# Two of a two-layer encoder's modulation vectors, moved: one from the attention to the channel mixer's first product, one from there to its second product

## Chip, cores and metric

The kernel runs on one core of a Trainium2 chip. The metric is device time in microseconds (us); the median of the runs is given. Batch 1, 1024 tokens, model width 1024, everything in float32. Matrix products are made exact to about float32 by splitting each operand into a high and a low part in a rounded format (`float32r`) and adding three products (high x high, high x low, low x high).

## The reference, cut to what matters

Two layers; layer 0 mixes tokens by forgetting attention, layer 1 by gated linear attention (GLA). Each layer has six modulation vectors of 1024 numbers, made from the one conditioning vector `c`:

```python
c_act = jax.nn.silu(c)
for i in range(DEPTH):
    mod = c_act @ ada_w[i] + ada_b[i]          # 1 x 6144, a 1024 x 6144 matrix per layer
    sh1, sc1, g1, sh2, sc2, g2 = jnp.split(mod, N_MOD, axis=-1)
    h = modulate(rms_norm(x, norm1_g[i]), sh1, sc1)
    y = mixer(h)                               # layer 0: attention, layer 1: GLA
    x = x + g1[:, None, :] * y
    h = modulate(rms_norm(x, norm2_g[i]), sh2, sc2)
    x = x + g2[:, None, :] * swiglu(h, ffn_w_in[i], ffn_w_out[i])
return rms_norm(x, final_g)
```

The vectors are numbered j = 0 to 5 in this order (shift, scale and gate of the token mixer, then shift, scale and gate of the channel mixer). Each is a product of one row with a 1024 x 1024 matrix, 4 MB of weights for very little arithmetic.

## The kernel before, in words

**Stages.** The kernel is one straight program: transposes and the first norm; the attention, by pairs of heads (eight pairs, `attention`), with the projections of the next pair woven in; the attention's output projection; layer 0's channel mixer; GLA; its output projection; layer 1's channel mixer; the last norm. TensorE (PE) carries the products, ScalarE (ACT) makes high parts and exponentials, VectorE (DVE) makes low parts, sums and maxima, GpSimd (POOL) scales and adds, and every DMA is issued from SyncE's queue (SP). Each engine works through its queue in order. The order in each queue is made by a scheduler at build time, from the order in which the program emits the operations and a simulated timeline.

**The channel mixer** (`ffn`, called for each layer) is made with a seven-product (Strassen) scheme. Its first product goes through 22 groups of columns; `prod` makes one of a group's seven block products. Its second product goes through three parts (`OC = 3`) of the hidden width, each with four column groups of seven products; `part` loads the hidden tiles of the next part from DRAM in between, and `late_raw` gives the buffers for those of them that have to be split into high and low parts on the chip (T3, T4). In the second product seven PSUM banks take results, which ScalarE or VectorE sums up (L1696, L1698).

**A modulation vector** is made by `ada_steps`, beside other work. With `nt` rows per partition a step loads a piece of the matrix by four DMAs (L423) and adds `nt` rows, each scaled by one number of `silu(c)`, onto an accumulator by VectorE (L442 the first, L444 the others, 128 x 256 each); after the last step TensorE sums over partitions (L449) and VectorE adds the bias (L452). With `nt` = 4 (attention) a vector has 8 steps of four operations and 32 DMAs of 128 KB; with `nt` = 2 (elsewhere) 16 steps of two operations and 64 DMAs of 64 KB. Either way it is 32 operations. `ahead` is how many steps are loaded in advance, which is the number of buffers less one; in the attention it is 0, with a ring of three buffers (`wr`) shared with the weights.

**When a step is emitted** is decided by a `Pace`: the surrounding code calls it with an amount of work just emitted (for instance `ada1(0.64 * n)` after each block product), and it emits steps until their stated costs have used the amount up. The cost of a step is 1.0 in the attention; elsewhere it is `ADA_A` between the load and the operations and `ADA_B` behind them. In the attention `ada0(3.3)` stands at the end of `qk_proj` for the head pairs from 2 on (12 calls). Before the change the vectors are made at these places:

- layer 0, vectors 0 and 1: before the attention, by other code
- layer 0, vectors 2, 3, 4, 5: attention
- layer 1, vectors 0 and 1: layer 0's channel mixer, first product (`mid`, three buffers)
- layer 1, vectors 2, 3, 4: GLA
- layer 1, vector 5: layer 1's channel mixer, first product

Other lines that are spoken of: L1138 adds the decay to the scores and takes the running extreme, L1142 the exponential, L1143 the reciprocal of the sum, L1144 the scaling of the probabilities, L1164 their transposes; L765, L767, L779 and L780 move projected queries and keys out of PSUM; L175 makes the low part of a weight block (`o_s`) or of probabilities; L286 to L288 are the three products of a split pair; L825 loads weights of the channel mixer, L1607 and L1597 hidden tiles.

Of the kernel before, what the change touches and what calls it, by code (L numbers as in the profile page):

```python
# [20 lines left out]
HALF = 512  # L21
# [32 lines left out]
def trunk(ctx, tc, x, c, ada_w, ada_b, norm1_g, norm2_g, ffn_w_in, ffn_w_out,  # L54
# [124 lines left out]
    opr_ = {}  # L179
# [131 lines left out]
    xr = Ring(big, take(8))  # L311
# [62 lines left out]
    for t in range(6):  # L374
        nt, src = (4, rows2[0:8, :]) if t < 4 else (2, crow)
# [35 lines left out]
    def ada_steps(l, j, acc, raw_of, nt, ahead):  # L411


        steps, got = deque(range(32 // nt)), deque()

        def load():
            if not steps:
                return
            n = steps.popleft()
            raw = raw_of([P, nt * 256], F32, f"ada{l}{j}{n}").rearrange("p (t c) -> p t c", t=nt)  # L420
            src = ada_w[l, 32 * nt * n:32 * nt * (n + 1), j * D:(j + 1) * D]
            for q in range(4):
                nc.sync.dma_start(raw[32 * q:32 * q + 32],  # L423
                                  src[:, 256 * q:256 * q + 256].rearrange("(r t) c -> r t c", t=nt))
            got.append(raw)

        for _ in range(ahead):
            load()
        for n in range(32 // nt):
            load()  # L430
            if ahead:
                yield ADA_A
            raw = got.popleft()
            with ExitStack() as es:
                if ahead:
                    es.enter_context(tc.issue_after(last_of("D")))
                elif n == 0:
                    es.enter_context(tc.issue_after(split_after["D"]))
                for t in range(nt):
                    o = (0 if nt == 4 else 32) + t * (32 // nt) + n  # L440
                    if n == t == 0:
                        nc.vector.tensor_scalar(acc, raw[:, t], c42[:, o:o + 1], None, op0=ALU.mult)  # L442
                    else:
                        nc.vector.scalar_tensor_tensor(acc, raw[:, t], c42[:, o:o + 1], acc,  # L444
                                                       op0=ALU.mult, op1=ALU.add)
            yield ADA_B if ahead else 1.0
        mp = pj([P, 2, 4], F32, f"mp{l}{j}")
        for b in range(2):
            nc.tensor.matmul(mp[:, b], acc[:, psl(b)], four, start=True, stop=True)  # L449
        o = l * 48 + j * 8  # L450
        qb = lambda t: t.rearrange("p (q b) -> p b q", b=2)
        nc.vector.tensor_add(qb(modc[:, l, j]), mp, qb(vec[:, o:o + 8]))  # L452
        for i, jj in ((0, 1), (1, 4)):
            if j == jj:
                make_a(l, i)
        yield 1.0
# [22 lines left out]

    ada0, ada1 = Pace(), Pace()  # L480

    def ada1_queue(js, acc, raws_):
        r = Cycle(raws_)
        for j in js:
            ada1.q.append(ada_steps(1, j, acc, r, 2, len(raws_) - 1))

    mk = mrows[2]
    nc.vector.memset(mk, 0.0)
# [608 lines left out]
    def qk_proj(p, i):  # L1097

        if i == 0:
            qkt[p] = qk_tiles(p)  # L1100
        wt = feed.next()
        feed.depth = 3
        for hf in range(2):
            ps = pj([P, HALF], F32, f"qk{i}{p}{hf}")
            yield from proj(ps, wt, hT, hf)
            (k_evac if i else q_evac)(ps, qkt[p], hf)
        if p > 1:
            ada0(3.3)

    oTs = {}  # L1110

# [108 lines left out]
            yield from g  # L1220

    acc0 = acc_r([P, 2, HALF], F32, "acc0")[:, 0, 0:256]
    for j in (2, 3, 4, 5):
        ada0.q.append(ada_steps(0, j, acc0, wr, 4, 0))
    run(v_half(0, 0, gates_end))
    q_evac(accs[1][1][1], qkt[0], 1)
# [76 lines left out]
    oh = new_h("oh")  # L1303
# [35 lines left out]
        def __init__(self, kind, i):  # L1339
            self.kind, self.i = kind, i  # L1340

    def ffn(l, oh, xs, slots, nm, mid, norm_end, each=None):

# [13 lines left out]
        b = {}  # L1357
# [217 lines left out]
        NSP = len(tsl) - 7 * OD  # L1575
        assert NSP == 3 * OD
        early_raw = Cycle([xs[k][:, hsl(hf)] for k in (6, 7) for hf in range(2)])
        late_raw = Cycle(list(tmpv) + [opr_["u"][0]])
        o = [{} for _ in range(OC)]
        ONAMES = ("B11", "T1", "T2", "T3", "B21", "T4", "B22")  # L1580

# [45 lines left out]
        def load_xr(i):  # L1627
            for a in range(2):
                for hf in range(2):
                    xr[(a, hf)] = late_raw()  # L1630
                    nc.sync.dma_start(xr[(a, hf)], x_sp[2 * i + a][:, hsl(hf)])

        nxt, n_nxt = [None], [0]
# [6 lines left out]
        for X in gs[2:]:  # L1640
            up = lambda n: advance(n) if X is gs[-1] else None
            if X is gs[-2]:
                ada1.flush()
                nxt[0] = part(0)
                advance(4)
            nc.scalar.copy(dest(X, C11), prod(feed.next(), B11))
            p5 = prod(feed.next(), T1)
            up(8)
            add(X, C12, prod(feed.next(), T2), C11)
            up(11)  # L1650
            add(X, C11, prod(feed.next(), B21))
            fin(X, C11)
            add(X, C22, prod(feed.next(), T3), C12)
            add(X, C12, p5)
            up(15)
            add(X, C21, prod(feed.next(), T4), C22)
            fin(X, C21)
            add(X, C22, p5)
            fin(X, C22)
            up(20)  # L1660
            add(X, C12, prod(feed.next(), B22))
            fin(X, C12)
            up(21)
# [4 lines left out]
            zs[i] = big.tile([P, 2, HALF], F32, tag=slots["to"][i], name=f"z{l}{i}")  # L1668
        for c_ in range(OC):
            last = c_ == OC - 1  # L1670
            n_nxt[0] = 0
            nxt[0] = last_part() if last else part(c_ + 1)
            for i in range(4):
                Y1, Y3 = (xs[2 * i][:, hsl(hf)] for hf in range(2))
                Y2, Y4 = (xs[2 * i + 1][:, hsl(hf)] for hf in range(2))
                Z1, Z5 = zs[i][:, 0], zs[i][:, 1]
                if last and i == 3:
                    feed.depth = 3

# [79 lines left out]
            marks["G0"] = last_of("G")  # L1759
        return gates  # L1760

    def mid(*js):
        v = Views(slots["hid"], 2, [HALF], f"ad{js[0]}").v
        ada1_queue(js, v[0][:, 0:256], v[1:4])

    ADA_A, ADA_B = 6.0, 3.0
    ffn(0, oh, xs, slots, "fo", lambda: mid(0, 1), norm_mixer)
    h1 = hs1
    after_norm = marks.pop("G0")
    split_after.update(marks)  # L1770
# [17 lines left out]
    athl = Ring(big, take(1))  # L1788
    s_slot, on_slot = take(2)
    ada_v = Views(take(2), 2, [HALF], "ad").v  # L1790
    ada1_queue((2, 3, 4), ada_v[0][:, 0:256], ada_v[1:3])
    ADA_A, ADA_B = 2.6, 1.0
    rm = ada_v[3]
    nc.vector.memset(rm, 1.0)
# [305 lines left out]
        return fzs[0]()  # L2100

    ADA_A, ADA_B = 12.0, 6.0
    ffn(1, oh, xs, slots, "go", lambda: mid(5), final_norm, final_scale)
    dump("xb1", xs)

# [28 lines left out]
```

## Time and profile before

| | |
|---|---|
| median of 3 runs | 2395.52 us (2395.1 to 2399.87) |
| the profiled execution's own time | 2397.77 us |
| its span, first to last instruction | 2396.1 us |
| mean granted clock of TensorE | 0.997 |
| data moved by DMA | 363.42 MB, 152 GB/s over the span |

The profile is of one execution, so sums are made against its 2397.77 us and then set against the median. In its lines a group is named by the line of the kernel, the engine, the operation, and output<-inputs by tile names without buffer numbers; PEld is TensorE's weight load, which overlaps its products. In a list of waits the numbers are us in total, times, longest. A wait for several things is put down to the one that came last. Matmuls overlap in the pipeline, so that their durations add up to more than TensorE's busy time.

### The profile page before, as it was taken

The numbers are of one execution on the slowest core, as the hardware profiler recorded it, in microseconds if no ns is written. First come the engines' busy times: TensorE is split into PE (matmuls) and PEld (weight loads), VectorE is DVE, ScalarE is ACT, GpSimd is POOL, SyncE is SP. The second block draws the span as 40 slices with busy tenths as digits, with TensorE's granted clock in tenths as the row PEclk, the third lists the DMA queues.
The fourth block names the chain that finished last, engine by engine and source line by source line (L and its number), as shares of the span: only waits on it lengthen the run. The fifth ranks groups of instructions, "written<-read, shape, count | busy, mean of one in ns | idle before, by whom it ended". The sixth has DMA issues, their size and how long they took to land.

```text
span 2396.1 us, 35784 instructions
## 1 busy us (share of the span) xinstructions
PE 2368.3 (99%) x12344; PEld 2016.8 (84%) x12344; DVE 1776.6 (74%) x3016; ACT 1127.8 (47%) x2164; POOL 1008.5 (42%) x911
## 2 busy tenths in 40 slices
PE   8999999999999999999999999999999999999998
PEld 7888888888888888888888888898888888888888
DVE  6577878886698788876798666655687877775787
ACT  6666555674443333345325645353343333345326
POOL 1333333333445666643264321222345666643262
PEclk9999999999999999999999999999999999999999
DMA  7422424342435544557655242334424544457664
GB/s 254 145 89 90 131 84 128 106 138 83 150 109 173 179 166 165 171 196 261 229 187 162 67 119 80 107 112 135 136 96 161 183 145 159 154 182 256 228 202 146
DMA packets 335773, 363.42 MB, mean 152 GB/s; under 512 B 24348, under 2 KB 277432, under 8 KB 335592
## 3 DMA queue, kind: packets, MB, share of 16 engines
q1 hardware_dynamic: 335592, 361.15, 45.9%
q8 instruction: 97, 1.59, 0.3%
q14 instruction: 84, 0.69, 0.1%
HBM read 268.19 MB, written 92.86 MB: 151 GB/s over the span
## 4 chain that ended last, share of the span: by engine, by line
PE 90%; DVE 5%; DMA 2%; ACT 1%; issue 1%; POOL 0%; SPq 0%; DVEq 0%; POOLq 0%; ACTq 0%
PE p_b L288 16%; PE p_b L286 16%; PE p_b L287 16%; PE t_b L1164 2%; PE o_b L1178 2%; PE qk_b L286 2%; PE qk_b L287 2%; PE qk_b L288 2%; PE vps_b L286 1%; PE vps_b L288 1%; PE vps_b L287 1%; PE s_b L1132 1%; PE s_b L1133 1%; PE gr_b L286 1%; PE gr_b L287 1%
## 5 line engine op out<-in xcount | busy, mean ns | idle before, releaser
L175 DVE TENSOR_TENSOR o_s<-xv_s,o_s 128x512 fp32r<-128x512 f32 (+1 forms) x376 | 324.1, 867 | 66.1 <-ACT o_s L174 65.6
L174 ACT CAST o_s<-xv_s 128x512 fp32r<-128x512 f32 (+1 forms) x376 | 216.2, 587 | 303.6 <-PE p_b L288 248.0
L287 PE MATMUL p_b<-B,o_s 128*128 128x512 f32 x608 | 237.8, 391 | 0.0
L288 PE MATMUL p_b<-B,o_s 128*128 128x512 f32 x608 | 237.5, 391 | 0.0
L286 PE MATMUL p_b<-B,o_s 128*128 128x512 f32 x608 | 236.3, 392 | 0.0
L1144 POOL TENSOR_SCALAR lp_s<-lp_s,st 128x128 f32<-128x128 f32 (+7 forms) x128 | 99.0, 778 | 291.1 <-DVE st L1143 280.7
L843 POOL TENSOR_TENSOR ex_s<-xv_s,xv_s 128x512 f32<-128x512 f32 (+1 forms) x64 | 85.5, 1335 | 292.8 <-DMA xv_s<-in_ffn_w_in_dram 120.7
L286 PE MATMUL p_b<-T,o_s 128*128 128x512 f32 x480 | 186.7, 389 | 0.0
L287 PE MATMUL p_b<-T,o_s 128*128 128x512 f32 x480 | 186.7, 389 | 0.0
L288 PE MATMUL p_b<-T,o_s 128*128 128x512 f32 x480 | 181.2, 389 | 0.0
L287 PEld LDWEIGHTS p_b<-B,o_s 128*128 128x128 f32 x608 | 115.0, 189 | 23.9
L286 PEld LDWEIGHTS p_b<-B,o_s 128*128 128x128 f32 x608 | 115.0, 189 | 23.8
L288 PEld LDWEIGHTS p_b<-B,o_s 128*128 128x128 f32 x608 | 114.7, 189 | 24.0
L1142 ACT ACTIVATE lp_s<-lp_s,st 128x128 f32<-128x128 f32 (+7 forms) x128 | 99.3, 777 | 65.2 <-DVE st L1138 62.1
L174 ACT CAST pt_s<-t_b 128x512 fp32r<-128x512 f32 (+1 forms) x160 | 79.7, 547 | 75.4 <-PE t_b L1164 73.9
L845 POOL TENSOR_TENSOR xv_s<-ex_s,xv_s 128x512 f32<-128x512 f32 (+1 forms) x64 | 88.1, 1377 | 60.7 <-DVE o_s L175 58.2
L1521 DVE TENSOR_TENSOR ex_s<-ex_s,p_b 128x512 f32<-128x512 f32 x140 | 93.7, 681 | 23.4 <-PE p_b L288 23.2
L227 POOL TENSOR_TENSOR w_l_s<-w__s,w_h_s 128x256 fp32r<-128x256 f32 x90 | 69.7, 803 | 94.7 <-ACT w_h_s L223 56.7
L175 DVE TENSOR_TENSOR pt_s<-t_b,pt_s 128x512 fp32r<-128x512 f32 (+1 forms) x160 | 96.2, 631 | 15.9 <-ACT pt_s L174 15.3
L287 PEld LDWEIGHTS p_b<-T,o_s 128*128 128x128 f32 x480 | 90.1, 188 | 18.7
L286 PEld LDWEIGHTS p_b<-T,o_s 128*128 128x128 f32 x480 | 90.1, 188 | 18.7
L288 PEld LDWEIGHTS p_b<-T,o_s 128*128 128x128 f32 x480 | 90.1, 188 | 18.6
(1954 smaller groups left out, 7392.9 us busy)
## 6 DMA issues: line engine op xcount, KB each, us to landing
xv_s<-in_ffn_w_in_dram SPq DMA_DIRECT2D x176, 256.0 KB, 3.3
hid_B<-x SPq DMA_DIRECT2D x70, 512.0 KB, 2.6
ad_s<-in_ada_w_dram SPq DMA_DIRECT2D x384, 64.0 KB, 2.4
hid_T<-x SPq DMA_DIRECT2D x36, 512.0 KB, 2.8
xv_s<-in_ffn_w_out_dram SPq DMA_DIRECT2D x96, 192.0 KB, 5.3
ada_s<-in_ada_w_dram SPq DMA_DIRECT2D x128, 128.0 KB, 2.8
xv_s<-in_ffn_w_out_dram SPq DMA_DIRECT2D x40, 256.0 KB, 2.9
T2o<-hid_T SPq DMA_DIRECT2D x18, 512.0 KB, 8.4
```

Source lines behind the costliest of these rows:

```text
L174: nc.scalar.copy(hi, src)
L175: nc.vector.tensor_sub(lo, src, hi.bitcast(F32))
L227: (nc.gpsimd if i < 3 else nc.vector).tensor_sub(lo[:, cs], rw[:, cs], hi[:, cs].bitcast(F32))
L286: nc.tensor.matmul(ps, ah, bh, start=start, stop=False)
L287: nc.tensor.matmul(ps, ah, bl, start=False, stop=False)
L288: nc.tensor.matmul(ps, al, bh, start=False, stop=stop)
L843: nc.gpsimd.tensor_add(s1, a21, a22)
L845: nc.gpsimd.tensor_sub(a11, s1, a11)
L1142: nc.scalar.activation(lp, lp, AF.Exp, bias=mcur, scale=-1.0, accum_out=st[:, qi, 2:3])
L1144: nc.gpsimd.tensor_scalar(lp, lp, st[:, qi, 3:4], 1.0, op0=ALU.mult, op1=ALU.mult)
L1164: nc.tensor.transpose(tp[:, i, :], lps[qi][:, psl(2 * b + jj)], ident)
L1521: nc.vector.tensor_add(d, d if src is None else dest(G, src), ps)
```

## The change

Layer 0's vector 5 (the gate of the channel mixer) goes from the attention's queue to the queue of layer 0's first product, layer 1's vector 1 from that queue to a new one in the second product, and the attention's pace goes from 3.3 to 2.4 a call. The new queue has one buffer and so loads nothing ahead; its accumulator and its buffer are the two halves of `opr_["u"]`, of which `late_raw` used one half before and no longer does (`load_xr`, later, uses it as before). It starts with the last two groups of the first product, at a pace of 5.0 and 2.5, and what is left is emitted before the last part of the second product. The conditions on `ahead` become conditions on `nt`, which is the same for all other vectors. `ffn` gets the new argument only for layer 0; the smaller `late_raw` holds in both layers.

```diff
-            if ahead:
+            if nt == 2:
                 yield ADA_A
...
-                if ahead:
+                if nt == 2:
                     es.enter_context(tc.issue_after(last_of("D")))
...
-            yield ADA_B if ahead else 1.0
+            yield ADA_B if nt == 2 else 1.0
...
-    def ada1_queue(js, acc, raws_):
+    def ada1_queue(ljs, acc, raws_):
         r = Cycle(raws_)
-        for j in js:
-            ada1.q.append(ada_steps(1, j, acc, r, 2, len(raws_) - 1))
+        for l, j in ljs:
+            ada1.q.append(ada_steps(l, j, acc, r, 2, len(raws_) - 1))
...
         if p > 1:
-            ada0(3.3)
+            ada0(2.4)
...
-    for j in (2, 3, 4, 5):
+    for j in (2, 3, 4):
         ada0.q.append(ada_steps(0, j, acc0, wr, 4, 0))
...
-        late_raw = Cycle(list(tmpv) + [opr_["u"][0]])
+        late_raw = Cycle(list(tmpv))
+        xr_raw = Cycle(list(tmpv) + [opr_["u"][0]])
...
             if X is gs[-2]:
                 ada1.flush()
+                if later:
+                    ada1_queue(later, opr_["u"][1][:, 0:256], opr_["u"][0:1])
+                    ada_rate(5.0, 2.5)
...
             last = c_ == OC - 1
+            if last:
+                ada1.flush()
...
-    ffn(0, oh, xs, slots, "fo", lambda: mid(0, 1), norm_mixer)
+    ffn(0, oh, xs, slots, "fo", lambda: mid((0, 5), (1, 0)), norm_mixer, later=((1, 1),))
```

More of the change, by code (lines that the diff above doesn't have):

```diff
@@ L1340, in __init__, with ffn @@
             self.kind, self.i = kind, i
-    def ffn(l, oh, xs, slots, nm, mid, norm_end, each=None):
+    def ffn(l, oh, xs, slots, nm, mid, norm_end, each=None, later=()):
         nonlocal pj, pin
@@ L1629, in load_xr @@
                 for hf in range(2):
-                    xr[(a, hf)] = late_raw()
+                    xr[(a, hf)] = xr_raw()
                     nc.sync.dma_start(xr[(a, hf)], x_sp[2 * i + a][:, hsl(hf)])
@@ L1760, in norm_mixer, with ada_rate, mid @@
         return gates
-    def mid(*js):
-        v = Views(slots["hid"], 2, [HALF], f"ad{js[0]}").v
-        ada1_queue(js, v[0][:, 0:256], v[1:4])
+    def ada_rate(a, b):
+        nonlocal ADA_A, ADA_B
+        ADA_A, ADA_B = a, b
+    def mid(*ljs):
+        v = Views(slots["hid"], 2, [HALF], f"ad{ljs[0][0]}").v
+        ada1_queue(ljs, v[0][:, 0:256], v[1:4])
     ADA_A, ADA_B = 6.0, 3.0
-    ffn(0, oh, xs, slots, "fo", lambda: mid(0, 1), norm_mixer)
+    ffn(0, oh, xs, slots, "fo", lambda: mid((0, 5), (1, 0)), norm_mixer, later=((1, 1),))
     h1 = hs1
@@ L1790, in trunk @@
     ada_v = Views(take(2), 2, [HALF], "ad").v
-    ada1_queue((2, 3, 4), ada_v[0][:, 0:256], ada_v[1:3])
+    ada1_queue([(1, j) for j in (2, 3, 4)], ada_v[0][:, 0:256], ada_v[1:3])
     ADA_A, ADA_B = 2.6, 1.0
@@ L2102, in trunk @@
     ADA_A, ADA_B = 12.0, 6.0
-    ffn(1, oh, xs, slots, "go", lambda: mid(5), final_norm, final_scale)
+    ffn(1, oh, xs, slots, "go", lambda: mid((1, 5)), final_norm, final_scale)
     dump("xb1", xs)
```

## The prediction, made before the result

> **What bounds the kernel now.** The page comes first, for the one engine that is never free, then a table of busy time by stage (the attention while vectors are made beside it, the first product of layer 0's channel mixer, its second product up to where the change would be done with it).
>
> ```profile
> span 2396.1 us, 35784 instructions
> ...
> PE 2368.3 (99%) x12344; PEld 2016.8 (84%) x12344; DVE 1776.6 (74%) x3016; ACT 1127.8 (47%) x2164; POOL 1008.5 (42%) x911
> ```
>
> ```profile
> core 0: us, PE busy (x) PEld busy (x) DVE busy (x) ACT busy (x) POOL busy (x), PEclk, DMA share, GB/s
> ...
> 137.00:474.00 337.00, 331.83 (x2170) 292.62 (x2169) 267.63 (x689) 204.21 (x437) 124.61 (x170) 1.00 0.35 109
> ...
> 700.00:1028.00 328.00, 328.00 (x1453) 271.63 (x1452) 270.61 (x355) 124.44 (x218) 203.70 (x137) 1.00 0.53 175
> 1040.00:1163.00 123.00, 123.00 (x544) 101.87 (x543) 79.42 (x112) 54.34 (x104) 48.20 (x40) 1.00 0.71 256
> ```
>
> TensorE (PE) is busy 99% of the span, so only its pauses can be won, 2396.1 - 2368.3 = 27.8 us in all. In the attention stretch it pauses 337 - 331.83 = 5.2 us. In the first product VectorE (DVE) is busier, 270.61 of 328 us (82%) against 267.63 of 337 (79%), and yet TensorE pauses for nothing there. So a high load of VectorE alone does not cost time; the place decides. What TensorE waited for in the attention stretch is the next view (us in total, times, longest).
>
> ```profile
> PE s_b L1132 <- DVE st L1138: 1.8, 3, 1.2
> PE t_b L1164 <- POOL lp_s L1144: 1.7, 1, 1.7
> PE vps_b L286 <- DVE QB L767: 1.2, 1, 1.2
> PE qk_b L286 <- DVE KLB L780: 0.3, 1, 0.3
> ```
>
> Three of the four name VectorE; together the four rows are 1.8 + 1.7 + 1.2 + 0.3 = 5.0 us. The fourth names GpSimd (POOL), so its moment has to be looked at, on VectorE and then on TensorE:
>
> ```profile
> 347.65 3.09 DVE L444 SCALAR_TENSOR_TENSOR acc_s<-ada_s,c,acc_s 128x256 f32<-128x256 f32 x6
> ...
> 353.52 0.49 DVE L444 SCALAR_TENSOR_TENSOR acc_s<-ada_s,c,acc_s 128x256 f32<-128x256 f32 x1 [1.43 <-DMA ada_s<-in_ada_w_dram]
> ...
> 354.91 0.16 DVE L1143 RECIPROCAL st<-st 128x1 f32<-128x1 f32 x1
> ```
>
> ```profile
> 356.24 0.55 PE L1164 MATMUL t_b<-ident,lp_s 128*128 128x128 f32 x3 [1.70 <-POOL lp_s L1144]
> ```
>
> Six modulation operations in a row hold VectorE for 3.09 us, then a seventh stands 1.43 us at the head of its queue for its own load; the reciprocal behind it is late, so GpSimd's scaling (L1144) is late, and TensorE stands 1.70 us. That is the mechanism that the change can act on: modulation work in VectorE's queue between the steps of a softmax, where a score has only a few us before TensorE needs it.
>
> **What goes from the attention.** One of four vectors: a quarter of the operations and loads in these rows (duration ns min/median/max).
>
> ```profile
> L423 SPq DMA_DIRECT2D ada_s<-in_ada_w_dram x128: 560/597/1381, 137.3 to 465.7; - x128
> L444 DVE SCALAR_TENSOR_TENSOR acc_s<-ada_s,c,acc_s x124: 460/485/1227, 142.5 to 473.3; 128x256 f32<-128x256 f32 x124
> L442 DVE TENSOR_SCALAR acc_s<-ada_s,c x4: 354/610/790, 142.2 to 403.6; 128x256 f32<-128x256 f32 x4
> ...
>   DMA ada_s<-in_ada_w_dram: 17.7, 13
> ```
>
> ```profile
> core 0: us, DVE busy (x), PEclk, DMA share, GB/s
> 137.00:474.00 337.00, 64.68 (x124) 1.00 0.35 109
> 700.00:1028.00 328.00, 36.69 (x62) 1.00 0.53 175
> ```
>
> 128 / 4 = 32 operations leave, at 64.68 / 124 = 0.52 us each 16.7 us of VectorE, and with them a quarter of its waiting for loads, 17.7 / 4 = 4.4 us. 21 us of VectorE are not 21 us of time: most lie under TensorE's 331.83 busy us. The three vectors that stay are also paced slower, 2.4 in place of 3.3 units a call, so a call sets off two or three steps of four operations in place of three or four. Bounds of the gain: nothing, if the remaining steps stall TensorE as often; and all of the 5.0 us, with, beyond it, a share of time hidden in stretched matmuls, of which the projection's rows against the product's give the size:
>
> ```profile
> L286 PE MATMUL qk_b<-h0h,w_h_s 128*128 128x512 f32 x224 | 91.7, 409 | 1.0 <-DVE QB L767 0.7 <-DVE KLB L780 0.3
> ```
>
> ```profile
> L286 PE MATMUL p_b<-T,o_s 128*128 128x512 f32 x480 | 186.7, 389 | 0.0
> ```
>
> (409 - 389) ns x 224 = 4.5 us, a quarter of it 1.1 us, so at most 6.1 us. A gain in proportion would be 5.0 / 4 = 1.25 us. I take 2.0, nearer to that than to all of it: the longest waits follow the longest runs, and the slower pace thins these too, but in the order of instructions of the changed kernel two runs of seven modulation operations are still in the attention, one of them behind the same kind of score steps. What is late next there is the softmax itself: once the queue is clear, TensorE's next limit is its own work.
>
> **What moves to the first product.** Its queue held layer 1's vectors 0 and 1 and now holds layer 0's vector 5 and layer 1's vector 0: the same 64 operations, 128 loads and two closing products. The vector moved there is needed only when the second product is gated, which is far behind. Nothing, both ways.
>
> **What the second product gets.** Layer 1's vector 1: 32 operations, 64 loads of half the size (two rows a step, not four: 32 more issues on SP than what left), one closing product that another stage loses. At the first product's 36.69 / 62 = 0.59 us the operations are 18.9 us. They run from the last two groups of the first product, some 123 us long at the pace written (16 steps of 7.5 units and one more). VectorE is free 123 - 79.42 = 43.6 us there, so 24.7 are left. The cover is TensorE's own stream; what would pierce it is VectorE falling behind by more than its lead. The lead is visible in what VectorE waited for in that stretch:
>
> ```profile
> DVE o_s L175 <- ACT o_s L174: 17.0, 13, 3.5
> DVE sg_s L1521 <- PE p_b L288: 4.8, 5, 2.0
> ```
>
> VectorE stands waiting for TensorE's finished products: it keeps no backlog. With seven accumulators in the second product, a few us of delay only fill banks.
>
> New is that this vector has one buffer and no load ahead, so each load waits for the step before it, and VectorE may wait for it at the head of its queue, with weight splits (L175) and sums (L1698) behind it. This wait does not occur in the trace of before in this stage; the nearest rows are the landings of the other vectors' loads (min/median/max us) and of what else is on the queues in these 123 us, and the load on DMA there:
>
> ```profile
> DMA to landing us min/median/max: 2.2/2.4/6.5
> ```
>
> ```profile
> xv_s<-in_ffn_w_out_dram SPq DMA_DIRECT2D x31, 192.0 KB, 6.3
> B11o<-hid_B SPq DMA_DIRECT2D x9, 512.0 KB, 8.4
> T2o<-hid_T SPq DMA_DIRECT2D x8, 512.0 KB, 10.2
> ```
>
> ```profile
> 1076.00:1094.00 18.00, 14.15 (x20) 1.00 1.04 396
> 1094.00:1112.00 18.00, 8.26 (x12) 1.00 0.70 239
> 1112.00:1130.00 18.00, 9.96 (x16) 1.00 0.36 112
> 1130.00:1148.00 18.00, 11.66 (x18) 1.00 1.02 388
> ```
>
> The columns of the last table are the stretch, VectorE's busy time, the clock, the share of DMA and GB/s.
>
> From the freeing of the buffer, four issues at the 0.597 us of the L423 row above (2.4 us) and a landing of 2.4 us make 4.8 us, less than the 7.5 between steps: no wait. Behind the hidden tiles' transfers, where DMA is at 1.04 or 1.02, a landing is rather the weights' 6.3 us: 8.7 us, a wait of 1.2 us. Even at all 16 steps that is 19 us, within the 24.7. So I take 0.2 us for the whole move, one short slip; bounds 0 and 16.1 us (the slower rival below). Below nothing it cannot go: no pause of TensorE in that stretch is left to win (123.00 of 123.00). A buffer less for the raw T3 and T4 tiles costs nothing: three are loaded ahead, into three.
>
> **Sum.** -2.0 + 0.2 = -1.8 us. The profiled execution took 2397.77 us, 1.7 outside the span; with the change 2396.0. The median of the runs shown, 2395.52, is 2.25 lower, so I forecast **2393.7**.
>
> **Rivals.**
>
> *All the stalls go.* The thinned steps never again meet a softmax at the wrong moment. For it: every wait in the list begins in or just behind modulation steps. Against it: the runs of seven that remain. It gives 2395.5 - 5.0 to 6.1 = 2389.4 to 2390.5, faster by a little over 0.2%.
>
> *Nothing comes of it.* TensorE loses the same pauses at other places, since the scheduler's order around the remaining steps is new; the operations leave but the waits stay. For it: only 5.0 us in eight separate waits stand to be won, and the gaps depend on where a step falls. It gives 2395.5 to 2398.
>
> *The single buffer starves VectorE* (the slower side). The place is the second product, the point from which it decides a mean landing of 7.5 + 24.7 / 16 - 2.4 = 6.6 us. If half of the steps meet the longest row, 10.2 us, these wait 10.2 + 2.4 - 7.5 = 5.1 us each: 8 x 5.1 + 18.9 - 43.6 = 16.1 us that TensorE stands, and the time is 2395.5 - 2.0 + 16.1 = 2409.6. For it: the share of DMA is 0.71 in that stretch. Against it: DMA is full in two spells only, with 0.70 and 0.36 between them, and VectorE enters each without a backlog. The Trainium skill (Trainium Kernel Development and Optimization, Best Practices) asks for double buffers so that transfers and compute overlap, which speaks against this part; by that rule alone every step would show its load. The attention's own row says that this is not so of loads issued just ahead of their use: 17.7 us in 13 waits over 32 steps.
>
> **How the numbers follow.** About 0.2% (4.8 us) is what a measurement of this kernel can tell from no change: faster is below 2390.7, slower above 2400.3. Forecast 0.60 and no effect 0.16 are both within it; all stalls gone 0.14 is faster; the starved VectorE 0.10 is slower. So 0.14, 0.76, 0.10. The range goes from the best bound, 2389.5, to 2401, over no effect and nearly half of the slower rival's price; what it leaves out is the rest of that rival.
>
> **What would show it.** In the attention, the operations at L442 and L444 down from 128 to 96, and TensorE's pauses there down from 5.2 to about 3 us. In the second product, 32 such operations on a tile named ex_s from about 1040 us on; VectorE's waits for their loads under 20 us in sum, and TensorE still at 123 of 123 us. Wrong, if waits of TensorE for o_s (L175) or for freed banks appear between 1040 and 1200 us, or if the attention's pauses do not shrink.

## The result, and the profile after

The changed kernel took 2410.03 us (median of 6 runs, 2402.45 to 2412.19) against 2397.06 us (6 runs) of the kernel before on the same chip: ratio 1.0049, 95% interval 1.0032 to 1.0066. It is slower, by half a per cent; the forecast was 2393.7, with a range up to 2401. The profiled execution took 2410.17 us, its span is 2408.4 us. In the file of the changed kernel the lines behind L1575 are a few higher: the hidden tiles' loads are L1598 and L1608, the sums of the second product L1702 and L1704.

The page of the changed kernel, busy time:

```profile
span 2408.4 us, 35809 instructions
...
PE 2373.7 (99%) x12344; PEld 2020.0 (84%) x12344; DVE 1777.4 (74%) x3016; ACT 1125.7 (47%) x2164; POOL 1005.6 (42%) x911
```

TensorE is idle 2408.4 - 2373.7 = 34.7 us, 6.9 more than before, but the span grew by 12.3: some of the loss is in busy time that has become slower. The table by stage says where (the columns are as in the prediction; the fourth row is the rest of the second product, the fifth the start of GLA):

```profile
core 0: us, PE busy (x) PEld busy (x) DVE busy (x) ACT busy (x) POOL busy (x), PEclk, DMA share, GB/s
137.00:474.00 337.00, 334.66 (x2186) 296.11 (x2185) 260.91 (x660) 204.76 (x438) 123.19 (x171) 0.99 0.31 98
700.00:1028.00 328.00, 328.00 (x1452) 271.67 (x1451) 268.13 (x352) 123.66 (x217) 203.46 (x138) 1.00 0.52 174
1040.00:1163.00 123.00, 121.84 (x537) 100.28 (x536) 85.78 (x131) 51.26 (x101) 41.17 (x34) 1.00 0.81 269
1163.00:1300.00 137.00, 130.35 (x571) 105.91 (x570) 114.82 (x170) 44.15 (x83) 60.74 (x50) 0.99 0.59 186
1300.00:1420.00 120.00, 114.39 (x692) 101.59 (x691) 78.45 (x134) 69.15 (x138) 39.04 (x42) 0.97 0.32 93
```

The attention's pauses fell from 5.2 to 337 - 334.66 = 2.3 us, and the first product has none, as forecast. The pauses are in the second product: 1.2 us in the first of its rows, 6.65 in the second. Measured in each trace from TensorE's first instruction of a stage to that of the next, the changed kernel stands to the one before like this (us): attention -1.97, first product 0.00, second product's first part +1.71, its **second part +7.93**, its third +1.61, GLA +3.81.

The waits of TensorE in the second product, from its timeline (start, duration, and in brackets the idle time before it with what ended it):

```profile
1168.60 0.50 PE L286 MATMUL p_b<-T1o,o032s_s 128*128 128x512 f32 x1 [1.50 <-ACT o032s_s L174]
1171.03 0.50 PE L288 MATMUL p_b<-T1o,o032s_s 128*128 128x512 f32 x1 [1.69 <-DVE o032s_s L175]
1189.04 0.58 PE L449 MATMUL mp_b<-four,ex_s 128*128 128x4 f32 x4 [1.80 <-DVE ex_s L444]
```

Two things are late: the high and low parts of one weight block (o032s), and the last operation of the late vector, for which its closing product stands at the head of TensorE's queue. The weight block comes from GpSimd's sum at L843. Before, and after (second fence):

```profile
1157.44 1.31 POOL L843 TENSOR_TENSOR ex_s<-xv_s,xv_s 128x384 f32<-128x384 f32 x1 [8.58 <-DMA xv_s<-in_ffn_w_out_dram]
```

```profile
1167.01 0.99 POOL L843 TENSOR_TENSOR ex_s<-xv_s,xv_s 128x384 f32<-128x384 f32 x1 [15.39 <-DMA xv_s<-in_ffn_w_out_dram]
```

GpSimd waited for the weights' load (xv_s, L825). Why that was late stands in SyncE's own timeline, before and after; a row with xN is a run of N issues, its duration from the first to the last:

```profile
1144.19 1.62 SPq L1607 DMA_DIRECT2D T2o<-hid_T  x2
1146.83 20.24 SPq L825 DMA_DIRECT2D xv_s<-in_ffn_w_out_dram  x9
```

```profile
1143.46 3.46 SPq L423 DMA_DIRECT2D ex_s<-in_ada_w_dram  x4
1147.03 1.66 SPq L825 DMA_DIRECT2D xv_s<-in_ffn_w_out_dram  x2
...
1158.17 0.38 SPq L825 DMA_DIRECT2D xv_s<-in_ffn_w_out_dram  x1
1159.42 3.77 SPq L423 DMA_DIRECT2D ex_s<-in_ada_w_dram  x4
1163.35 3.16 SPq L825 DMA_DIRECT2D xv_s<-in_ffn_w_out_dram  x3
```

Before, SyncE is done with the hidden tiles at 1146 us and issues weights as their buffers come free. After, it still has hidden tiles to issue up to 1157 us, and four small loads of the vector stand between the weights. How much SyncE was ahead can be read from its waits between 1060 and 1168 us: the time for which it stood at a weights' load because the buffer was still in use. Before, and after:

```profile
SPq L825 <- DVE o_s L175: 38.5, 17, 9.3
```

```profile
SPq L825 <- DVE o_s L175: 3.2, 2, 2.4
```

38.5 us of slack on SyncE's queue became 3.2. In these 108 us SyncE issued 117 DMAs against 80; the instructions took 55.8 against 31.9 us, 23.9 of it for 40 loads of the vector, and the waits 51.6 us (all rows of that view). That the queue is occupied for 107.4 of the 108 us is nothing new, since before it was 31.9 + 74.9 = 106.8 us; new is that it no longer stands there because it is ahead.

### The profile page after: what moved, and what is told of

It is laid out like the page before. It is cut to its first block, busy times and chain, and to the rows that moved or that the text cites. A ratio compares the mean times of both kernels' runs of the same rounds, so it can differ in the third digit from the quotient of the medians.

```text
span 2408.4 us, 35809 instructions
## 1 busy us (share of the span) xinstructions
PE 2373.7 (99%) x12344; PEld 2020.0 (84%) x12344; DVE 1777.4 (74%) x3016; ACT 1125.7 (47%) x2164; POOL 1005.6 (42%) x911
## 4 chain that ended last, share of the span: by engine, by line
PE 84%; DVE 6%; DMA 5%; ACT 2%; issue 2%; POOL 1%; SPq 0%; DVEq 0%; POOLq 0%; ACTq 0%
PE p_b L286 14%; PE p_b L288 14%; PE p_b L287 14%; PE o_b L1178 2%; PE t_b L1164 2%; PE qk_b L286 2%; PE qk_b L287 2%; PE qk_b L288 2%; PE vps_b L288 1%; PE s_b L1132 1%; PE vps_b L286 1%; PE vps_b L287 1%; PE s_b L1133 1%; PE gr_b L286 1%; PE gr_b L287 1%
## 5 line engine op out<-in xcount | busy, mean ns | idle before, releaser
L843 POOL TENSOR_TENSOR ex_s<-xv_s,xv_s 128x512 f32<-128x512 f32 (+1 forms) x64 | 85.4, 1334 | 291.9 <-DMA xv_s<-in_ffn_w_in_dram 124.5
L1521 DVE TENSOR_TENSOR ex_s<-ex_s,p_b 128x512 f32<-128x512 f32 x140 | 93.6, 680 | 24.0 <-PE p_b L288 23.9
```

What stands on the lines that cost most here:

```text
L843: nc.gpsimd.tensor_add(s1, a21, a22)
L1521: nc.vector.tensor_add(d, d if src is None else dest(G, src), ps)
```

## Experiments

Each kernel was timed in five rounds beside the kernel before, the kernels of one group on one chip; the kernel before took 2399.82, 2397.62, 2398.51 and 2397.67 us in the four groups and 2398.25 beside e1. In the tables are the differences of stages to the profile of before (us; parts 1 to 3 are those of the second product), the median, and the ratio to before with its 95% interval. The stages come from one execution each. How far they scatter is seen where a kernel leaves a stage as it was: a3 and b3 show +0.5 and -0.5 in the attention, and b3 shows -1.6 in the first product, because TensorE's clock was 0.95 and 0.88 from 650 to 670 us in the trace of before, with TensorE busy throughout, and 1.00 in b3's. A single difference under 2 us says little.

### First group: which part of the change

*a1* is the changed kernel again. *a2* puts all three vectors into the first product:

```diff
-    ADA_A, ADA_B = 6.0, 3.0
-    ffn(0, ..., lambda: mid((0, 5), (1, 0)), norm_mixer, later=((1, 1),))
+    ADA_A, ADA_B = 4.2, 2.1
+    ffn(0, ..., lambda: mid((0, 5), (1, 0), (1, 1)), norm_mixer)
```

*a3* leaves the attention as before (four vectors, 3.3) and only puts layer 1's vector 1 into the second product (`mid((1, 0),)`). *a4* loads once for the late vector and uses that piece in all 16 steps: all 32 operations, 4 loads in place of 64, so that its vector is not the right one (nor is it in b2, c2 and d3 below, which leave out operations or half of the data).

> The changed kernel itself, timed beside the others on one chip. All theories expect what was measured, 10 to 13 us over the kernel before (+0.4 to +0.55%). In the profile the attention should end about 2 us earlier than before and the first layer's second product should lose 8 to 10 us.

> The attention's part of the change alone: three vectors left there at pace 2.4, and the other two of layer 1 and the gate of layer 0 all in the first product (three buffers, pace 4.2 and 2.1 so that three fit), none in the second. Theory 'single buffer' (VectorE stands for loads that have no load ahead): 2 us faster than before (2395), with no wait of TensorE in the first product. Rival 'work' (VectorE's extra 19 us themselves cost, whereever they are added to the channel mixer): the first product goes from 82% to 88% busy on VectorE and loses several us, the time is 2 to 8 us over before.

> The second product's part alone: the attention keeps four vectors at pace 3.3, the first product keeps one vector of layer 1, the second product gets the other. If the whole loss is in the second product and the attention's part is a gain of 2 us, this is 2 us slower than the changed kernel, 12 to 15 us over before. Rival 'attention' (the loss comes from the attention's new order): as fast as before within 2 us.

> The changed kernel with only the first step's load of the vector in the second product; its other 15 steps compute on the same data (so this vector is wrong, and with it layer 1's scale). All 32 operations stay. Theory 'single buffer': the loss in the second product is gone, and the time is about 2 us under before. Rival 'work': the loss stays, 8 us or more over before. Rival 'loads' (the 60 loads hold up SP's queue and the DMA engines, whatever VectorE does): gone as well; the next call tells it from the first theory.

| kernel | attention | first | part 1 | part 2 | part 3 | GLA | median | ratio (interval) |
|---|---|---|---|---|---|---|---|---|
| a1 the change | -2.6 | 0.0 | +2.3 | +7.5 | +1.4 | +2.5 | 2406.56 | 1.0027 (1.0016 to 1.0038) |
| a2 three in the first product | -2.2 | +7.3 | 0.0 | 0.0 | -0.6 | +0.1 | 2401.86 | 1.0010 (1.0001 to 1.0018) |
| a3 second product only | +0.5 | -0.5 | +1.1 | +6.5 | +1.2 | +3.9 | 2409.11 | 1.0047 (1.0034 to 1.0061) |
| a4 operations without loads | -2.8 | 0.0 | 0.0 | +0.5 | -0.6 | +0.2 | 2393.86 | 0.9978 (0.9969 to 0.9987) |

The loss belongs to the move into the second product (a3), and the attention's part is a gain of 2 to 3 us in every kernel that has it. a4 settles one point: 32 more operations on VectorE in that stage cost nothing, so the prediction's cover for them held. What costs is the loads, or what they do to VectorE. a2 shows the other end: in the first product VectorE goes from 270.61 to 294.29 of 328 us, and TensorE pauses for it:

```profile
PE p_b L286 <- DVE sg_s L1521: 3.4, 2, 2.1
```

### Second group: the single buffer, the loads, the smaller ring

*b1* gives the late vector two buffers and one load ahead; *b2* keeps all its 64 loads and leaves out 31 of its 32 operations; *b3* is the kernel before with three raw buffers for T3 and T4 instead of four.

```diff
-    ada1_queue(later, opr_["u"][1][:, 0:256], opr_["u"][0:1])
+    ada1_queue(later, sm.tile([P, 256], F32, tag="t1k", name="lacc"), opr_["u"])   # b1
```

> The changed kernel with two buffers and one load ahead in the second product (the accumulator is moved to another tile to make room). Same work, same loads. Theory 'single buffer': VectorE's 33 us of standing for these loads fall below 8 us, TensorE's pauses in the second product fall from 7 to 10 us to under 2, and the time is 0 to 2 us under before. Rival 'work' and rival 'loads': as slow as the changed kernel, 8 us or more over before.

> The changed kernel with all loads of the vector in the second product, but only the first of its 32 operations (the vector is wrong, and with it layer 1's scale). Nothing on VectorE waits for the other loads. Theory 'single buffer': the loss is gone, 0 to 2 us under before. Rival 'loads': the loss stays, 6 us or more over before. Rival 'work': gone as well.

> The kernel before with only the smaller ring of buffers for the raw hidden tiles (three in place of four, in both layers), which is a part of the change. Expected: no difference, within 1.5 us. Rival: the tiles come late and the second products of both layers lose some us each.

| kernel | attention | first | part 1 | part 2 | part 3 | GLA | median | ratio (interval) |
|---|---|---|---|---|---|---|---|---|
| b1 two buffers | -3.1 | 0.0 | +1.0 | +10.6 | -0.6 | +0.6 | 2406.33 | 1.0036 (1.0022 to 1.0049) |
| b2 loads alone | -2.5 | +0.7 | 0.0 | +0.3 | -0.6 | +0.1 | 2396.14 | 0.9993 (0.9984 to 1.0002) |
| b3 three raw buffers | -0.5 | -1.6 | 0.0 | 0.0 | -0.6 | -0.3 | 2396.55 | 0.9992 (0.9983 to 1.0000) |

The theory of the single buffer falls with b1. VectorE's waits for the vector's loads (1040 to 1210 us), in the changed kernel and in b1:

```profile
DVE ex_s L444 <- DMA ex_s<-in_ada_w_dram: 33.3, 12, 6.4
```

```profile
DVE lacc L444 <- DMA ex_s<-in_ada_w_dram: 8.0, 2, 4.8
```

Three quarters of the waiting are gone, and the second part loses 10.6 us in place of 7.5 to 7.9. In b1 the same weight block is late: TensorE waits 1.8 us for it, GpSimd's sum starts at 1167.92 us. Part of the 10.6 is the clock: it stood at 0.50 from 1171.3 to 1181.6 us, and TensorE, busy for 9.07 us of these, lost half of that, 4.5 us. Neither the operations (a4) nor the loads alone (b2) cost anything measurable, but b2 is at the edge: SyncE's slack before weights is 1.2 us there, and GpSimd's sum for that block starts at 1164.23 us, where the changed kernel had 1167.01, b1 1167.92 and before 1157.44. So I formed a third theory: SyncE's queue, in which the weights stand behind the small loads.

### Third group: issues, bytes or buffer

*c1* loads each step of the late vector by one DMA, *c2* brings only the first of each load's two rows, *c3* issues the loads from ScalarE's queue, *c4* makes one DMA a step of every vector in the kernel.

```diff
-            for q in range(4):
-                nc.sync.dma_start(raw[32 * q:32 * q + 32],
-                                  src[:, 256 * q:256 * q + 256].rearrange("(r t) c -> r t c", t=nt))
+            nc.sync.dma_start(raw, src.rearrange("(r t) (q c) -> q r t c", t=nt, q=4))      # c1, c4
+                nc.sync.dma_start(raw[32 * q:32 * q + 32, 0], s_[:, 0])                     # c2
+                nc.scalar.dma_start(raw[32 * q:32 * q + 32], ...)                           # c3
```

> The changed kernel, but each step of the late vector is loaded by one DMA of 256 KB in place of four of 64 KB: 16 issues in place of 64, the same bytes in the same 1 KB pieces, the same single buffer. In the changed kernel SyncE's queue issues only about 10 to 12 DMAs in 10 us while the transfers are full, whatever their size, and the weights behind the 64 small ones are 8 to 11 us late in the second product's second part, which lost 7.5 to 7.9 us. Theory 'issues': 48 issues fewer at about 1.3 us bring the weights forward by most of that lag, so that the second part loses under 1.5 us; time 2394 to 2398, ratio 0.998 to 1.000. Rival 'bytes' (4 MB more at 390 GB/s are 10.8 us of full transfers, in however many pieces): the lag stays at 8 us or more, the second part loses 6 or more; ratio 1.002 to 1.005. Rival 'single buffer' (VectorE stands for a load that is not ahead): its waits shrink only by the issue time of three DMAs a step, at 1.3 us and over 6 or 7 steps in full spells; second part still loses 4 or more.

> The changed kernel, but each of the 64 loads of the late vector brings only the first of its two rows (32 KB), which both operations read, so this vector is wrong: as many issues, operations and waits, half the bytes (2 MB). Theory 'issues': nothing is gained on SyncE's queue; second part still loses 5 to 9 us, ratio 1.002 to 1.005. Rival 'bytes': the lag is halved to some 5 us, which the weights' lead of about 8 us covers; second part loses under 1.5, ratio 0.998 to 1.000. 'Single buffer': as 'issues', since landing times are set by the other transfers.

> The changed kernel, but the 64 loads of the late vector are issued from ScalarE's queue, not SyncE's, where the weights and hidden tiles are. Theory 'issues': the weights are no longer behind them; their issue times are within 3 us of those of the kernel without these loads and the second part loses under 1.5 us, unless ScalarE, which is busy 51 of 123 us there but now stands at a load until VectorE has freed the buffer, is late with the high parts of weights (a loss of its own, seen as waits for L174 on ScalarE's side). Time 2394 to 2399. Rival 'bytes': the same 10.8 us of transfers, second part loses 6 or more, ratio 1.002 to 1.005. 'Single buffer': VectorE still stands for its loads; second part loses 5 or more.

> The changed kernel with one DMA a step for every vector, in all stages (in the attention 512 KB in place of four of 128 KB). 'Issues': as with the late vector alone or a little better, since the first product and GLA have fewer small issues ahead of weights too (GLA lost 2.5 to 3.8 us by a weight load that landed late behind such loads): 2392 to 2397, ratio 0.997 to 0.9995. 'Bytes': 1.002 to 1.005. A load of 512 KB lands later than one of 128 KB, so in the attention, where nothing is loaded ahead, VectorE may wait longer and up to 3 us of what was won there may be given back.

| kernel | attention | first | part 1 | part 2 | part 3 | GLA | median | ratio (interval) |
|---|---|---|---|---|---|---|---|---|
| c1 one DMA a step | -3.0 | +6.3 | +10.7 | +26.7 | -0.6 | +2.5 | 2438.79 | 1.0169 (1.0155 to 1.0183) |
| c2 half the bytes | -3.0 | +0.8 | 0.0 | +6.8 | -0.6 | 0.0 | 2401.37 | 1.0018 (1.0009 to 1.0027) |
| c3 ScalarE's queue | -2.9 | +1.0 | +9.1 | +6.5 | +3.4 | +0.3 | 2420.47 | 1.0089 (1.0075 to 1.0103) |
| c4 one DMA everywhere | +82.3 | +19.1 | +10.9 | +26.8 | -0.5 | +45.8 | 2588.10 | 1.0792 (1.0776 to 1.0809) |

None of the theories foresaw the size of c1's loss: the edit was meant to take away issues and made a far slower load. In the attention of c4, where the share of DMA is 0.28, VectorE's longest wait for such a load is 9.7 us:

```profile
DVE acc_s L442 <- DMA ada_s<-in_ada_w_dram: 93.1, 16, 9.7
```

(18.4 us in 11 waits in the changed kernel.) In c1 SyncE itself stood for them, with the weights behind it:

```profile
SPq L423 <- DMA ex_s<-in_ada_w_dram: 35.0, 9, 6.8
```

So c1 and c4 say nothing on the number of issues. c3 is spoiled too: ScalarE, which works in order, stood at loads that waited for VectorE, and TensorE paused 5.0 us behind ScalarE's sum (L1702) and 4.1 behind its high part (L1381). c2 seems to speak against the bytes: half of them, and the second part still loses 6.8 us. But it does not part the bytes from the issues, since an issue of one row took a median of 0.379 us in place of 0.567. The weights came in time, and one long pause was left, that of the closing product:

```profile
PE mp_b L452 <- DVE ex_s L447: 3.2, 1, 3.2
PE p_b L286 <- DVE sg_s L1524: 0.4, 1, 0.4
```

A pause of 3.2 us, and 6.8 lost. The table of TensorE in stretches of 6 us shows the rest, for c2 and then for the changed kernel (busy us and matmuls, granted clock, DMA share, GB/s):

```profile
core 0: us, PE busy (x), PEclk, DMA share, GB/s
1164.00:1170.00 6.00, 6.00 (x27) 1.00 0.26 70
1170.00:1176.00 6.00, 2.81 (x13) 0.88 0.42 107
1176.00:1182.00 6.00, 6.00 (x17) 0.56 0.27 79
1182.00:1188.00 6.00, 6.00 (x28) 1.00 0.43 112
```

```profile
1164.00:1170.00 6.00, 3.83 (x16) 1.00 0.81 160
1170.00:1176.00 6.00, 4.97 (x15) 0.72 0.36 108
1176.00:1182.00 6.00, 6.00 (x28) 1.00 0.39 113
1182.00:1188.00 6.00, 5.23 (x24) 1.00 0.26 72
1188.00:1194.00 6.00, 4.96 (x24) 1.00 0.66 181
```

28 matmuls go into 6 us when nothing is wrong. In c2 30 were made in the 12 us around the pause, four of them the closing product's own small ones (128x4), so 26 of 56: 30 x 6 / 28 = 6.4 us lost for 3.2 of pause, since the clock was at 0.50 from 1174.5 to 1181.3 us while TensorE was busy again. In the changed kernel the two waits for o032s, 3.2 us together and close to one another, do the same: 31 of 56 matmuls, 5.4 us, with the clock at 0.50 from 1171.4 to 1174.9 us. The closing product's 1.8 us alone (1182 to 1194) cost 12 matmuls, 2.6 us, its own four counted out, at full clock. The Trainium skill (TensorE: Matmul & The Clock Gate, Part 1) describes a gate that halves the clock after an idle window of about 3.4 us and opens after a busy one. Here the low stretches lasted 3.4 us or a multiple of it (3.41 in the changed kernel, 6.83 in c2, 10.24 in b1), but the length of a pause did not decide alone. The clock fell behind pauses of 2.0 us in b1 (1.8 and 0.2), 2.3 in a3 (0.7 and 1.7) and the 3.2 above, and in the trace of before at 659 us behind none; it stayed at 1.00 behind 1.7 us in d2 (below) and, in GLA, behind 3.0 us in d4 (below). What decides is not shown.

### Fourth group and last run: half the issues, the closing product, the place

*d1* makes the late vector in 8 steps of four rows, the attention's form: four DMAs of 128 KB, 32 in all, the same 4 MB, still one buffer and nothing ahead. *d2* emits the closing product after the first column group of the last part. *d3* is c2 with the same move. *d4* starts the late vector in the first product, behind the two others, which go faster, with two buffers. *e1* joins d1 and d4.

```diff
+    ada1.q.append(ada_steps(1, 1, lacc, lambda *_: opr_["uu"], 4, 0, True)); ada_rate(10.0, 5.0)   # d1
...
+                if last and i == 1 and held:                    # d2, d3
+                    held.pop()()
...
-    ADA_A, ADA_B = 6.0, 3.0
+    ADA_A, ADA_B = 5.0, 2.5      # d4, and behind it the late vector at (6.5, 3.0)
+    ADA_A, ADA_B = 5.5, 2.75     # e1, and behind it four-row steps at (13.0, 6.0)
```

> The changed kernel, but the late vector goes by 8 steps of four rows (four DMAs of 128 KB and four operations a step, the form of the attention, at twice the cost a step) in place of 16 steps of two: 32 issues on SyncE's queue in place of 64, the same 4 MB, one buffer of twice the size. Theory 'issues': half the lag of the weights goes (from 11 to 15 us down to some 6 us, against the kernel without these loads), TensorE's waits for o032s go, and the second part loses only what the closing product costs: total 2396 to 2402, ratio 0.999 to 1.0025. Rival 'bytes': the lag stays at 10 us or more and the waits for o032s (about 3 us) stay; ratio 1.003 to 1.006.

> The changed kernel, but the closing product of the late vector and its bias (L449, L452) are emitted in the last part, after its first column group, not right behind the vector's last operation. TensorE's wait of 1.8 us for ex_s at L449 must go; the waits for o032s (3.2 us and the low clock behind them) stay. So about 1.8 us come back and no more: ratio 1.002 to 1.0045. If the wait for the closing product is only a shadow of the late weights, nothing comes back.

> The kernel with half the bytes a load for the late vector (its second row is the first again, so this vector is wrong), with the closing product moved as in the run before. With half the bytes the closing product was the only pause in the second part, 3.2 us, and that part lost 6.8. If the rest, 3.6 us, is the low clock behind this one pause, then all 6.8 us come back: 2392 to 2396, ratio 0.997 to 0.999. If the 3.6 us are something else (transfers, VectorE), only 3.2 us come back: ratio 1.000 to 1.001.

> The changed kernel with the late vector begun earlier: the two vectors of the first product go at 5.0 and 2.5 units a step in place of 6.0 and 3.0, and the late one follows at once at 6.5 and 3.0 with two buffers (both halves of the tile, its sums in another), so that it ends by about 1095 to 1110 us, ahead of the full spell from 1126 on. If its loads in that spell and its end behind them are the cause, the second part loses under 1 us and the attention's 2 to 3 us remain: 2393 to 2396, ratio 0.997 to 0.9995. Against it: with all three vectors in the first product, VectorE was late there and 7.3 us were lost; here about 84 operations are in it against 96, so up to 3 us could be lost there, ratio up to 1.0005.

> The changed kernel with the late vector both in four-row steps (32 issues) and begun early: the first product's two vectors at 5.5 and 2.75 units a step, the late one right behind them at 13 and 6 a step of four rows. If the issues on SyncE's queue were the cause, nothing is lost in the second product (under 1 us over its three parts), up to 1.2 us in the first product by VectorE's higher load; the attention's 2 to 4 us remain: 2393 to 2396, ratio 0.9975 to 0.9995. If something else in the second product were at work, as much as with four-row steps alone, 0.9985 to 1.0005.

| kernel | attention | first | part 1 | part 2 | part 3 | GLA | median | ratio (interval) |
|---|---|---|---|---|---|---|---|---|
| d1 32 issues | -4.5 | 0.0 | +1.1 | +1.3 | -0.5 | +1.2 | 2395.62 | 0.9993 (0.9983 to 1.0003) |
| d2 closing later | -2.1 | 0.0 | +1.6 | +2.2 | +5.1 | 0.0 | 2404.77 | 1.0027 (1.0016 to 1.0038) |
| d3 half bytes, closing later | -2.2 | +1.0 | 0.0 | +2.5 | +3.0 | -0.2 | 2402.22 | 1.0015 (1.0006 to 1.0023) |
| d4 begun earlier | -4.1 | +1.2 | +1.3 | 0.0 | -0.6 | +1.2 | 2396.86 | 0.9994 (0.9986 to 1.0002) |
| e1 both | -2.7 | +2.7 | 0.0 | +0.5 | -0.6 | +1.2 | 2398.74 | 1.0005 (0.9996 to 1.0014) |

d1 speaks for the issues, against the bytes, and once more against the buffer. Its loads land much later than the changed kernel's; the summary lines of the vector's issues in d1 and in the changed kernel:

```profile
L426 SPq DMA_DIRECT2D ex_s<-in_ada_w_dram x28: 560/567/742, 1046.6 to 1157.2; - x28
...
DMA to landing us min/median/max: 2.7/8.3/10.0
```

```profile
L423 SPq DMA_DIRECT2D ex_s<-in_ada_w_dram x60: 560/567/1413, 1049.9 to 1185.1; - x60
...
DMA to landing us min/median/max: 2.2/3.2/8.2
```

A median landing of 8.3 us against 3.2, with a single buffer, and the loss of the second part is 1.3 us in place of 7.9. An issue takes SyncE 0.567 us whether it brings 64 or 128 KB, so the bytes are the same and the time of issuing is halved. Counting the issues' own time and the waits of SyncE before them, the vector's loads held the queue between 1060 and 1168 us for 41.8 us in the changed kernel, 42.0 in b1 and 29.3 in d1. The weights are back at their places (those of the late block are issued from 1150 us, its sum starts at 1160.26), SyncE's slack before weights is 10.8 us, and VectorE waits no longer than in b1:

```profile
1150.17 2.36 SPq L828 DMA_DIRECT2D xv_s<-in_ffn_w_out_dram  x3
1153.44 4.35 SPq L426 DMA_DIRECT2D ex_s<-in_ada_w_dram  x4
1158.01 8.12 SPq L828 DMA_DIRECT2D xv_s<-in_ffn_w_out_dram  x3
```

```profile
DVE lacc L447 <- DMA ex_s<-in_ada_w_dram: 8.6, 2, 7.0
```

b1 and d1 are the pair to compare: the same waits of VectorE (8.0 and 8.6 us, two each), 64 issues against 32, +10.6 against +1.3 us. It is not a perfect pair: d1's last load goes out at 1157.2 us, b1's at 1166.2 (the changed kernel's at 1185.1), and 4.5 of b1's 10.6 us are the clock.

d2 took the closing product's wait away as expected, and one of the two waits for o032s went with it; with 1.7 us of pause left the clock stayed at 1.00 and the second part lost 2.2. But the last part, where VectorE is busy 51.83 of 58 us even before, lost 5.1 us, so little came back in all. d3 missed: its own pause went, but the weights were late again (1.8 us), with the same half bytes as c2, which had had them just in time. Half the bytes do not give the queue enough slack. d4 and e1 show the place: with most of the loads ahead of the full spell, the second part loses 0.0 and 0.5 us, and SyncE's slack before weights is 25.4 and 20.0 us. Yet e1, expected at 0.9975 to 0.9995, came out at 1.0005. What the attention wins, 2 to 4 us, is then spent in part or whole in the first product and GLA. No version with the whole computation beats the kernel before by more than the measurement can tell.

## Why the prediction was wrong, point by point

- **The attention: right.** 96 operations, pauses 2.3 us ("about 3"), gain 2.0 us by the trace of the changed kernel, as forecast; 2.0 to 4.5 in all kernels that have this part (c4 apart), against +0.5 and -0.5 us in the two that haven't (a3, b3).
- **The first product: right.** 0.00 us for the exchanged vector. That more would not fit was shown by a2.
- **A buffer less for T3 and T4: right**, 0.9992 (b3).
- **The second product, +0.2: this is the step that failed**, where it says "Even at all 16 steps that is 19 us, within the 24.7. So I take 0.2 us for the whole move". The cover was worked out for VectorE, and for VectorE it held (a4). The move's 64 issues were counted ("32 more issues on SP than what left") and priced at nothing. They are 64 x 0.567 = 36 us of SyncE's queue, in a stage in which it had 38.5 us of slack in 108, and the weights (L825) stand behind them. In these 108 us 40 of them held the queue for 41.8 us with their waits, and the slack fell by 35.3. Measured: +1.7, +7.9 and +1.6 us in the three parts.
- **"4.8 us, less than the 7.5 between steps: no wait" failed too.** The sum began with issues that go out as soon as the buffer is free. On a full queue they do not: VectorE waited 33.3 us in 12 waits, where under 20 were forecast, although the landings, median 3.2 us, were well under the 6.6 from which the slower rival was to decide. It cost little by itself (b1 took three quarters of it away and won nothing), except in the closing product's 1.8 us.
- **The slower rival** named the place and gave 2409.6 against 2410.03 measured, but by another mechanism, so that the match is a coincidence. Its point of decision, a mean landing of 6.6 us, is refuted: at a median of 3.2 us the time was lost. (d1's 8.3 us are no second test, since its steps are twice as far apart: by the same sum its point is 15 + 24.7 / 8 - 2.4 = 15.7 us.)
- **A miscount:** the rival by which nothing comes of it speaks of "eight separate waits" in the attention; the four rows have 3 + 1 + 1 + 1 = 6. Nothing in the sum hangs on it.
- **What was not in the sum:** the clock. A stall was priced at its length; 3.2 us of it cost 5.4. And GLA, +3.8 us: ScalarE stood 5.79 us at a weights' load, before 3.18, and the norm behind it was late, so that TensorE paused 3.0 us (`gr_b`, waiting for `gvt_s`) and the clock fell again:

```profile
1322.55 1.14 ACT L223 CAST w_h_s<-w__s 128x512 fp32r<-128x512 f32 x2 [5.79 <-DMA w__s<-in_gla_w_in_dram]
```

It shows in the changed kernel, its repeat, a3 and c1. In d4 and e1 the pause is as long (3.0 and 2.8 us), but the clock stayed at 1.00 and GLA lost 1.2; d1 lost 1.2 with a pause of 0.9. The others show no loss (under 0.7), c4 apart. Why that load is late is left open.

Also open is how the lateness on SyncE's queue divides. Of the 41.8 us, 23.9 are the issues' own time, 8.5 standing until an earlier transfer has landed and 9.4 standing for VectorE; standing for landings at all other loads was 24.4 us, before 23.5. In d1 the three are 14.0, 7.7 and 7.6. And a full queue is not the whole story: in b2 the loads hold it for 40.4 us and leave 1.2 us of slack, but the sum of the late block starts 2.8 us earlier than in the changed kernel, and the second part loses only 0.3. What gives it these 2.8 us is not shown.

## What to carry to other kernels

Before loads are moved into a stage, read the issuing queue like an engine: count the issues times the duration of one, and look for the time for which the queue stands waiting for free buffers, which is its slack; what stands behind the new loads pays when that is used up. Many small loads can use up the queue while DMA still has room (its share was 0.81 here), so make them fewer, in a form whose landing has been seen. And price a stall of TensorE by the clock behind it: single pauses of 1.7 and 1.8 us cost 2.2 and 2.6 us, but 3.2 us of pause cost 5.4 and 6.4 where the clock fell.

## What the runs showed of the hardware that was not expected

- An issue on SyncE takes as long for 64 as for 128 KB (0.567 us), 0.38 for a weights' load of 192 KB and for one row of the vector (32 KB). By the waits in the traces it also stands until an earlier transfer has landed: 32.9 of the 108 us in the changed kernel, 23.5 before.
- Four DMAs of 32 partitions each are much faster than one of four dimensions for the same bytes and pieces: with one DMA for each step in all vectors the kernel took 2588.10 us, 1.0792 times before. Which of the transfer engines it used was not looked at.
- The granted clock fell to 0.5 behind 3.2 us of pause, with TensorE busy again, and was back after 6.8 us. Other stretches at 0.5 lasted 3.4 us (the changed kernel) and 10.2 us (b1), and a pause of 3.0 us (d4, in GLA) brought none on:

```profile
1172.00:1174.00 2.00, 0.20 (x1) 1.00 0.48 111
1174.00:1176.00 2.00, 0.60 (x3) 0.63 0.09 25
1176.00:1178.00 2.00, 2.00 (x6) 0.50 0.49 139
1178.00:1180.00 2.00, 2.00 (x6) 0.50 0.00 0
1180.00:1182.00 2.00, 2.00 (x8) 0.67 0.33 98
1182.00:1184.00 2.00, 2.00 (x11) 1.00 0.33 98
```

(The kernel with half the bytes, c2, in stretches of 2 us.)
